# First-layer scores: three half-height products on two 64-row tiles, two query tiles at a time, instead of two full-height products

## The chip, the core and the metric

The kernel runs on one core of a Trainium2 chip. The metric is device time in microseconds (us) of one execution. The engines are named as the profile names them: PE (TensorE matmuls), PEld (TensorE weight loads), DVE (VectorE), ACT (ScalarE), POOL (GpSimd) and SP (SyncE, whose queue issues every DMA here).

## What is computed

Two layers of a decoder trunk on 2048 tokens of width 1024, in float32. Each layer is `x + W_out(mixer(RMSNorm(x)) * silu(gate))`. Layer 0, which the change touches, is stick-breaking attention with 16 heads of width 64; layer 1 is latent attention with 8 heads. The mixer of layer 0, cut to what matters:

```
z = einsum('bthd,bshd->bhts', q, k) * scale          # scores, contracted over d = 64
mask = s_idx < t_idx
log_fail = where(mask, log_sigmoid(-z), 0)
later = cumsum(log_fail, reverse) - log_fail
a = where(mask, exp(log_sigmoid(z) + later), 0)
o = einsum('bhts,bshd->bthd', a, v)
```

## The kernel before

**Exact parts.** The result must be close to float32, and the PE takes each number as a "high" part (the number rounded to the PE's fp32r type) and a "low" part (what is left). A product of two numbers is then built from products of parts. `split` (L432) makes both parts from a bank of PSUM: ACT writes the high part, DVE subtracts it and writes the low part. `HLS` (L374) names the three products that are kept, high*high, high*low and low*high; `unit` (L486) uses them for the projections.

**Stages of layer 0.** `proj0` (L539) computes, for a pair of heads `hp` (8 pairs) and a group `j` of 512 tokens (4 groups), the query, key, value and gate projections with 24 products of 512 columns each. `attn0` (L589) does the attention of one such stage: for each of the two heads it walks the key groups g from j down to 0, and in each the four query tiles `rt` of 128 rows. In the diagonal group (g = j) tile rt needs (rt + 1) * 128 key columns, in the others all 512. There are 64 diagonal and 96 other (head, j, g) blocks, so 640 tiles of scores. For each tile: the score products into a PSUM bank `z` (3 banks), two sigmoids on ACT (L606, L607; the second one overwrites z), a scan along the row on DVE that reads z (L610 or L613), a product on POOL (L615), transposes on the PE into bank `t` (L625), and a split into `at` (L627). After four tiles come the products with the values into bank `av` (L632).

**The scores before.** For a head, `qd` (L552) holds the query's high part in all 128 partitions (64 computed, 64 copied by a DMA, L556) and likewise its low part; `ks` (L558) holds the key's high part in one half of the partitions and its low part in the other half. So one product with a full 128-row contraction gives q_part * k_high + q_part * k_low, and two of them give all four products of parts:

```
z = bank("z")
with sched.group():
    for l in range(2):
        C.mm(z[:, :W], qd[:, h, l, rt * P:(rt + 1) * P], ks[:, h, :W], l == 0, l == 1, W)
```

**Order.** Nothing is written in its final order. The code records instructions, and `Sched.issue` (L185) puts them in an order per engine: it takes, again and again, the instruction that by its own table of durations can start first, among those whose inputs are ready and whose buffers are free. Instructions of one `group` are issued together. `proj0` of the next stage gets priorities that spread it over `attn0` of the current one (L710), so that the PE's queue mixes projection products with attention. The engines then run these orders as they stand, each waiting at the head of its own queue.

**Buffers around it.** The normalised inputs `xn` of a stage (8 slices of 512 KB) come from DRAM through a ring of `XB` = KD + 2 = 10 buffers (L496); in the last projection of a stage the loads for the next one are recorded, two at once and then one after each slice (L573 to L579). During the last attention stage the eight slices of the output weights `wo` are loaded and split (L708), the first 512-token group's `y` is loaded, and the first output tiles are computed between the attention's instructions. Tiles of `x` come in as `xr` (L796). At the layer's other border, eight slices `xk` are loaded for layer 1's input projections; three of them have their own ring `xk0` (L820), five take the place of the output weights.

Of the kernel before, what the change touches and what calls it, by code (L numbers as in the profile page):

```python
# [20 lines left out]
P = 128  # L21
# [10 lines left out]
class Ref:  # L32
    """A view of a buffer that is resolved when its instruction is issued."""

# [28 lines left out]
class Buf:  # L63
    """A tile; with a ring it gets its slot when the first instruction that uses it is issued."""

# [17 lines left out]
class Pool:  # L83
    """A pool that opens over the pools `below`, once the work in the pools `after` has been issued."""

# [30 lines left out]
class Ring:  # L116
    """The slots of a tag, taken in the recorded order; another may go ahead if it leaves `spare` slots free."""

# [9 lines left out]
class Sched:  # L128
    """Puts the recorded instructions in an issue order: each engine takes the first that can run."""

# [11 lines left out]
    def add(self, eng, dur, call, outs, ins):  # L142
        """One instruction; those of a group are issued together."""
        op = self.cur
        if not isinstance(op, Op):
            op = Op()
            op.eng, op.dur, op.calls, op.deps, op.succ, op.bufs = eng, 0.0, [], set(), [], []
            op.idx = op.prio = len(self.ops)
            op.ready = 0.0
            op.lat = self.LAT[eng]  # L150
            self.ops.append(op)
            if self.cur is not None:
                self.cur = op
        op.dur += dur
        op.calls.append(call)
        for refs, write in ((ins, False), (outs, True)):
            for r in refs:
                b = r.buf
                hit = lambda box: all(x0 < y1 and y0 < x1 for (x0, x1), (y0, y1) in zip(box, r.box))  # noqa: E731
                for box, o in b.writes:  # L160
                    if o is not op and hit(box):
                        op.deps.add(o)
                if write:
                    for box, o in b.reads:
                        if o is not op and hit(box):
                            op.deps.add(o)
                if b.ring is not None and b not in op.bufs:
                    op.bufs.append(b)
                    b.left += 1
                    b.ring.pool.left += 1  # L170
                (b.writes if write else b.reads).append((r.box, op))
        return op
# [7 lines left out]
    def spread(self, a, b, lo, hi):  # L180
        """The instructions a..b get priorities that lie evenly between those of lo and hi."""
        for i in range(a, b):
            self.ops[i].prio = lo + (i - a + 0.5) / max(b - a, 1) * (hi - lo)
# [104 lines left out]
class Chip:  # L288
    """The instructions in use, recorded with what they take."""

# [68 lines left out]
    def select(self, x, base, fill):  # L359
        """Keeps x where row + base >= column."""  # L360
        self.s.add("pool", 300.0,
# [16 lines left out]
def trunk(ctx: ExitStack, tc: tile.TileContext, x, w0, wo0, g0, g1, wlat, wgate, gqa, gkva,  # L378
# [33 lines left out]

# [1 line left out]
    ident = const.tile([P, P], F32, "ident")  # L414
    identb = const.tile([P, P], BF16, "identb")
    sched.add("pool", 1000.0, lambda: make_identity(nc, R(ident)), refs(ident), [])
    def causal(dst, base, fill):
        """0 where the column comes before the row (or is at it, base 0), else `fill`."""
        mtmp = pa.tile([P, G], F32, "tmp", 2)[:, 0:P]
# [10 lines left out]

# [1 line left out]
    def split(hi, lo, src, n=G, gain=None):  # L432
# [17 lines left out]
    def norm_scale(pl, xts, jtag, jbufs, mixed=False):  # L450
        """x / rms(x); mixed: with all engines, where nothing else runs."""
        for i in range(4):
# [33 lines left out]
    def unit(acc, w, xk, n=G, after=None):  # L486
        """acc += w^T x over the model width, in three products of exact parts."""
        for k in range(KD):
# [5 lines left out]

# [1 line left out]
    XB = KD + 2  # L496
    ws, kv, xq, cur = {}, {}, {}, {}
# [23 lines left out]
    def load_x(j):  # L521
# [3 lines left out]
        else:  # L525
            xts = [pk.tile([P, D], F32, ("ks", "vv")[i % 2], 5).all() for i in range(4)]
        for i in range(4):
# [11 lines left out]
    def proj0(n):  # L539
# [11 lines left out]
        acc = mul(0)  # L551
        qd = pk.tile([P, 2, 2, G], F32R, "qd", 2)  # L552
        for h in range(2):
            lo_, hi_ = slice(64 * h, 64 * h + 64), slice(64 - 64 * h, 128 - 64 * h)
            split(qd[lo_, h, 0, :], qd[lo_, h, 1, :], acc[lo_, :])
            C.dma(qd[hi_, h].bitcast(F32), qd[lo_, h].bitcast(F32), 256)  # L556
        acc = mul(1)
        ks = pk.tile([P, 2, G], F32R, "ks", 5)  # L558
        for h in range(2):
            lo_, hi_ = slice(64 * h, 64 * h + 64), slice(64 - 64 * h, 128 - 64 * h)  # L560
            split(ks[lo_, h, :], ks[hi_, h, :], acc[lo_, :])
        acc = mul(2)
# [26 lines left out]
    def attn0(hp, j):  # L589
        qd, gt = cur[hp, j]  # L590
        y = pa.tile([P, G], F32, "y")
        for h in range(2):
            av = bank("av")
            prev = {}
            for g in range(j, -1, -1):
                ks, vv = kv[hp, g]
                diag = g == j
                at = pa.tile([P, 2, 4, G], F32R, "at", 2)
                for rt in range(4):
                    W = (rt + 1) * P if diag else G  # L600
                    z = bank("z")
                    with sched.group():
                        for l in range(2):
                            C.mm(z[:, :W], qd[:, h, l, rt * P:(rt + 1) * P], ks[:, h, :W], l == 0, l == 1, W)
                    a = pa.tile([P, G], F32, "a", 5)
# [83 lines left out]
    for n, (hp, j) in enumerate(stages):  # L689
# [11 lines left out]
        else:  # L701
            qy = pk.tile([P, 2, 2, G], F32R, "qd", 2)
            parts = [pk.tile([P, 2, G], F32R, t, 5).all() for t in ("ks", "vv")] + [qy[:, 0], qy[:, 1]]
            for k in range(KD):
                t = parts[k] if k < 4 else pm.tile([P, 2, G], F32R, "y", 4).all()
                C.dma(t.bitcast(F32), y_d[0, :, k], 512)
                yts[0, k] = t
            load_wo(pm, wo0, 0, KD, G // 2, 3)  # L708
            a1 = a0 + int(LAST * (a1 - a0))
# [3 lines left out]

# [1 line left out]
    def out_proj(i, yt, xt, after=None, order=range(KD), dst=None):  # L715
        """x += y wo; with dst the halves of the width go one after the other, each to DRAM as soon as it is there."""
        acc = [bank("pj" if i % 2 == 0 else "z") for _ in range(2)]
# [44 lines left out]
    sk = pb.tile([P, NT, 64], F32, "sk")  # L762

    def prep():
        C.dma(gq_n, gqn, 1)
# [22 lines left out]
    for j in range(NG):  # L788
        done = []
        for i in range(4):  # L790
            t = 4 * j + i
            if t == 1:
                early = [yts[0, k] for k in range(KD)]
                for k in range(4):
                    yts[0, k] = load_y(pl, y_d, 0, k, "y", 4)
            xt = (pl if t else pm).tile([P, D], F32, "xr", 6 if t else 1)  # L796
            C.dma(xt, x[t * P:(t + 1) * P, :], 512)
# [81 lines left out]

# [1 line left out]
    ISQ = 1.0 / math.sqrt(QK1)  # L881
# [34 lines left out]

    def proj1(n):  # the first stages also take the banks that attention leaves free at that time
        h, j = stages[n]
# [142 lines left out]

# [1 line left out]
    pf = sb("pf", "right", (pw1,))  # L1063
# [89 lines left out]
```

## Time and profile before

| | us |
|---|---|
| median of 3 runs | 3069.71 (3065.83 to 3071.62) |
| span of the profiled execution | 3068.7 |
| PE busy in it | 2993.4 |
| PEld busy | 2490.3 |
| DVE busy | 2020.7 |
| ACT busy | 1871.9 |
| POOL busy | 1493.9 |

The median lies 1.0 us above the span of the profiled execution. Layer 0's projections and attention take the first half of the span, to about 1590 us; then come layer 0's output projection, layer 1's input projections (to about 2030 us), layer 1's attention and its output projection. A busy share of the PE tells that matmuls were in flight, not that it ran at its peak; how far apart matmuls of a kind start is read from the timeline.

### The profile page before, as it was taken

Reading aid. Unit: us, or ns where it says so; the run is one execution under the profiler, and the core shown is the slowest. Engines: PE = TensorE matmul, PEld = TensorE weight load, DVE = VectorE, ACT = ScalarE, POOL = GpSimd, SP = SyncE. Lnnn points to the kernel's source line nnn. Section 1 sums busy time; section 2 is a strip of 40 time slices with the busy share of each in tenths; the row PEclk is TensorE's granted clock in tenths of the full one; section 3 lists DMA queues with packets and bytes.
Section 4 is the critical chain, followed back from the end, with each engine's and each line's share of the span. In section 5 each row is a group of like instructions: output and inputs, shape, how many; then the busy total and the mean of one; then the engine's idle time right before and its main releaser. Section 6 shows DMA issues by size and latency. Waiting matters only on the chain.

```text
span 3068.7 us, 48665 instructions
## 1 busy us (share of the span) xinstructions
PE 2993.4 (98%) x15856; PEld 2490.3 (81%) x15856; DVE 2020.7 (66%) x3427; ACT 1871.9 (61%) x4635; POOL 1493.9 (49%) x2931
## 2 busy tenths in 40 slices
PE   8899999999999999999989999989999999999999
PEld 6678888888888888888778888878888888888787
DVE  5777896978869778787863231147777777778511
ACT  5676786867768677786852132257776776777300
POOL 4664664756647565574652120136455455455200
PEclk9899999999999999999999999999999999999999
DMA  6253434344243342433339672142232232223462
GB/s 240 103 172 124 131 104 140 108 138 148 84 147 103 124 152 88 147 121 116 117 121 325 244 276 108 72 157 80 78 95 68 88 103 67 69 80 93 162 216 103
DMA packets 134797, 399.88 MB, mean 130 GB/s; under 512 B 16656, under 2 KB 39696, under 8 KB 131984
## 3 DMA queue, kind: packets, MB, share of 16 engines
q1 hardware_dynamic: 134544, 396.76, 38.4%
q8 instruction: 127, 2.08, 0.3%
q14 instruction: 126, 1.03, 0.1%
HBM read 272.97 MB, written 98.57 MB: 121 GB/s over the span
## 4 chain that ended last, share of the span: by engine, by line
PE 78%; DVE 10%; ACT 5%; issue 3%; POOL 2%; DMA 2%; SPq 0%; DVEq 0%; POOLq 0%; ACTq 0%
PE pj L297 30%; PE z L297 22%; PE av L297 12%; PE t L301 10%; DVE pp L342 3%; PE t L297 3%; PE pj L301 1%; DVE at L319 1%; DVE nm L349 1%; ACT a L312 1%; DVE qs L329 1%; POOL s L329 1%; ACT s L312 1%; DVE y L319 1%; DVE pt L319 1%
## 5 line engine op out<-in xcount | busy, mean ns | idle before, releaser
L297 PE MATMUL pj<-xn,w 128*128 128x512 f32 x3072 | 864.2, 402 | 2.0 <-DVE qd L319 1.9
L319 POOL TENSOR_TENSOR a<-a,pp 128x512 f32<-128x512 f32 (+3 forms) x640 | 612.8, 960 | 475.1 <-DVE pp L342 443.3
L297 PEld LDWEIGHTS pj<-xn,w 128*128 128x128 f32 x3072 | 545.8, 189 | 100.2 <-issue 3.7
L342 DVE TENSOR_TENSOR_SCAN pp<-z,cy,a 128x512 f32<-128x512 f32 x384 | 484.2, 1274 | 43.8 <-ACT z L312 40.8
L312 ACT ACTIVATE at<-t 128x512 fp32r<-128x512 f32 (+3 forms) x640 | 341.0, 535 | 156.9 <-PE t L301 155.0
L319 DVE TENSOR_TENSOR at<-t,at 128x512 fp32r<-128x512 f32 (+3 forms) x640 | 377.7, 599 | 83.6 <-ACT at L312 78.4
L312 ACT ACTIVATE a<-z 128x512 f32<-128x512 f32 (+3 forms) x640 | 335.6, 535 | 117.6 <-PE z L297 101.4
L297 PE MATMUL z<-ks,qd 128*128 128x512 f32 (+3 forms) x1280 | 366.1, 377 | 13.6 <-DVE pp L342 9.5
L297 PE MATMUL av<-at,vv 128*128 128x512 f32 (+3 forms) x1280 | 376.7, 379 | 2.1 <-DVE at L319 2.1
L301 PE MATMUL t<-ident,a 128*128 128x128 f32 x2176 | 344.9, 274 | 8.4 <-POOL a L319 3.6
L301 PEld LDWEIGHTS t<-ident,a 128*128 128x128 f32 x2176 | 272.8, 141 | 82.6 <-POOL a L319 7.2
L312 ACT ACTIVATE z<-z 128x512 f32<-128x512 f32 (+3 forms) x640 | 337.9, 535 | 0.7
L329 POOL TENSOR_SCALAR s<-s,c,ri 128x512 f32<-128x512 f32 (+3 forms) x280 | 200.6, 730 | 164.9 <-DVE ri L353 122.6
L297 PEld LDWEIGHTS z<-ks,qd 128*128 128x128 f32 x1280 | 225.2, 190 | 67.0 <-DVE pp L342 21.5
L297 PE MATMUL av<-pt,vv 128*128 128x512 f32 (+2 forms) x960 | 268.6, 386 | 5.5 <-DVE pt L319 5.3
L312 ACT ACTIVATE s<-z,nm 128x512 f32<-128x512 f32 (+2 forms) x320 | 199.9, 626 | 119.3 <-DVE nm L349 112.5
L297 PE MATMUL z<-knt,qn 128*128 128x512 f32 (+2 forms) x960 | 258.8, 378 | 6.8 <-ACT s L312 6.4
L319 DVE TENSOR_TENSOR pt<-t,pt 128x512 fp32r<-128x512 f32 (+1 forms) x312 | 182.8, 606 | 110.9 <-ACT pt L312 108.4
L297 PEld LDWEIGHTS av<-at,vv 128*128 128x128 f32 x1280 | 223.8, 190 | 38.5 <-DVE at L319 5.5
L342 DVE TENSOR_TENSOR_SCAN pp<-z,later 128x128 f32<-128x128 f32 (+3 forms) x256 | 204.2, 814 | 47.6 <-ACT z L312 30.5
L349 DVE TENSOR_REDUCE nm<-z 128x1 f32<-128x512 f32 (+2 forms) x320 | 190.7, 604 | 38.8 <-PE z L297 37.5
L312 ACT ACTIVATE pt<-t 128x512 fp32r<-128x512 f32 (+1 forms) x312 | 162.0, 533 | 66.4 <-PE t L301 64.6
(234 smaller groups left out, 4940.1 us busy)
## 6 DMA issues: line engine op xcount, KB each, us to landing
xn<-xn_d SPq DMA_DIRECT2D x224, 512.0 KB, 4.8
xn_d<-xn SPq DMA_DIRECT2D x64, 512.0 KB, 3.8
y_d<-yh SPq DMA_DIRECT2D x64, 512.0 KB, 2.6
y<-y_d SPq DMA_DIRECT2D x60, 512.0 KB, 5.0
qd<-qd SPq DMA_DIRECT2D x64, 256.0 KB, 3.0
xk<-xn_d SPq DMA_DIRECT2D x32, 512.0 KB, 6.2
cqt<-c_d SPq DMA_DIRECT2D x16, 1024.0 KB, 5.1
ckv<-c_d SPq DMA_DIRECT2D x32, 512.0 KB, 3.6
```

The lines of the kernel that those rows point to most:

```text
L297: lambda: self.nc.tensor.matmul(R(out), lhsT=R(l), rhs=R(r), start=start, stop=stop),
L301: self.s.add("pe", 109.0, lambda: self.nc.tensor.transpose(R(out), R(src), R(ident)), refs(out), refs(src, ident))
L312: self.nc.scalar.activation(R(out), R(src), func, **kw)
L319: self.s.add(eng, ns, lambda: self.eng[eng].tensor_tensor(out=R(out), in0=R(a), in1=R(b), op=op), refs(out), refs(a, b))
L329: self.s.add(eng, ns, lambda: self.eng[eng].tensor_scalar(out=R(out), in0=R(a), scalar1=R(s1), scalar2=R(s2), op0=op0, op1=op1), refs(out) ...
L342: lambda: self.nc.vector.tensor_tensor_scan(R(out), R(a), R(b), initial=R(init), op0=ALU.mult, op1=op),
L349: lambda: self.nc.vector.tensor_reduce(out=R(out), in_=R(src), axis=AX.X, op=op, **kw),
```

## The change

The scores use two 64-row tiles of the PE's array. `qd` now holds, for even query tiles, both parts of the query in partitions 0 to 63, and for odd query tiles in partitions 64 to 127. `ks` holds both parts of the key in the lower 64 partitions and again in the upper 64; so it is twice as large, and the copying DMA is now that of `ks`. For each pair of query tiles two banks `z` are taken, and six products of 64 rows are issued in one group: for each of the three of `HLS`, one of the lower tile for the even query tile and one of the upper tile for the odd one. The query's parts are split by four instructions of 256 columns per part instead of two of 512. The product low*low is no longer formed.

To make room, the ring of `xn` has 9 buffers instead of 10; the last slice of `wo` is no longer loaded with the others but into two buffers of `xk0`, once the pools of the attention are closed; and the first tile `xr` comes from that later pool too.

```
@@ layer 0 @@
-    XB = KD + 2
+    XB = KD + 1
...
@@ proj0 @@
         acc = mul(0)
-        qd = pk.tile([P, 2, 2, G], F32R, "qd", 2)
+        qd = pk.tile([P, 2, 2, 2, P], F32R, "qd", 2)
+        av_ = acc.all().rearrange("p (a b t) -> p a b t", a=2, b=2)
+        for h in range(2):
+            for b in range(2):
+                r_ = slice(64 * b, 64 * b + 64)
+                split(qd[r_, h, 0], qd[r_, h, 1], av_[64 * h:64 * h + 64, :, b, :], G // 2)
+        acc = mul(1)
+        ks = pk.tile([P, 2, 2, G], F32R, "ks", 5)
         for h in range(2):
             lo_, hi_ = slice(64 * h, 64 * h + 64), slice(64 - 64 * h, 128 - 64 * h)
-            split(qd[lo_, h, 0, :], qd[lo_, h, 1, :], acc[lo_, :])
-            C.dma(qd[hi_, h].bitcast(F32), qd[lo_, h].bitcast(F32), 256)
-        acc = mul(1)
-        ks = pk.tile([P, 2, G], F32R, "ks", 5)
-        for h in range(2):
-            lo_, hi_ = slice(64 * h, 64 * h + 64), slice(64 - 64 * h, 128 - 64 * h)
-            split(ks[lo_, h, :], ks[hi_, h, :], acc[lo_, :])
+            split(ks[lo_, h, 0], ks[lo_, h, 1], acc[lo_, :])
+            C.dma(ks[hi_, h].bitcast(F32), ks[lo_, h].bitcast(F32), 256)
         acc = mul(2)
...
@@ attn0 @@
+                zs = {}
                 for rt in range(4):
                     W = (rt + 1) * P if diag else G
-                    z = bank("z")
-                    with sched.group():
-                        for l in range(2):
-                            C.mm(z[:, :W], qd[:, h, l, rt * P:(rt + 1) * P], ks[:, h, :W], l == 0, l == 1, W)
+                    if rt % 2 == 0:
+                        zs = {r: bank("z") for r in (rt, rt + 1)}
+                        with sched.group():
+                            for n, (lq, lk) in enumerate(HLS):
+                                for r in (rt, rt + 1):
+                                    w = (r + 1) * P if diag else G
+                                    p = slice(64 * (r % 2), 64 * (r % 2) + 64)
+                                    C.mm(zs[r][:, :w], qd[p, h, lq, r // 2, :], ks[p, h, lk, :w], n == 0, n == 2, w / 2)
+                    z = zs[rt]
...
@@ last stage @@
-            load_wo(pm, wo0, 0, KD, G // 2, 3)
+            load_wo(pm, wo0, 0, KD - 1, G // 2, 3)
...
@@ layer 0 out @@
+    wo[KD - 1] = [[], []]
+    for n in range(2):
+        part = pb.tile([P, 2, G], F32R, "xk0", 3)
+        for c in range(0, G, G // 2):
+            raw = pm.tile([P, G // 2], F32, "woraw", 3)
+            C.dma(raw, wo0[:, KD - 1, n * G + c:n * G + c + G // 2], 128)
+            split_sb(part[:, 0, c:c + G // 2], part[:, 1, c:c + G // 2], raw, G // 2, "dve" if c else "pool")
+        for b in range(2):
+            wo[KD - 1][b].append(part[:, b, :])
...
-            xt = (pl if t else pm).tile([P, D], F32, "xr", 6 if t else 1)
+            xt = pl.tile([P, D], F32, "xr", 6)
```

The built program has 16496 matmuls instead of 15856. 1920 of them are 64-row products; they stand in the PE's queue in 320 runs of six, each with full-height matmuls before and behind it.

The PE's queue late in layer 0's attention, in the stage before the last (z: scores, t: transposes, av: products with the values, pj: projections, `ident` the identity of a transpose). Before:

```order
L297 MATMUL pj<-xn,w 128x512 x3
L301 MATMUL t<-ident,a 128x128 x4
L297 MATMUL pj<-xn,w 128x512 x3
L297 MATMUL av<-at,vv 128x512 x2
L301 MATMUL t<-ident,a 128x128 x4
L297 MATMUL av<-at,vv 128x512 x2
L297 MATMUL z<-ks,qd 128x512 x2
L297 MATMUL av<-at,vv 128x512 x2
```

Now:

```order
L301 MATMUL t<-ident,a 128x128 x4
L297 MATMUL z<-ks,qd 128x512 x6
L297 MATMUL pj<-xn,w 128x512 x3
L301 MATMUL t<-ident,a 128x128 x4
L297 MATMUL pj<-xn,w 128x512 x3
L297 MATMUL av<-at,vv 128x512 x2
L297 MATMUL pj<-xn,w 128x512 x3
L297 MATMUL av<-at,vv 128x384 x2
```

Where two products of one query tile stood, six products of two query tiles stand, with as much other work between one such group and the next.

The PE's queue at the end of layer 0's attention, from the last products with the values (`wo`: slices of the output weights; z and pj are here banks of the output projection). Before:

```order
L297 MATMUL z<-wo,y 128x512 x6
L297 MATMUL av<-at,vv 128x512 x2
L297 MATMUL z<-wo,y 128x512 x6
L297 MATMUL pj<-wo,y 128x512 x6
L297 MATMUL z<-wo,y 128x512 x6
L297 MATMUL pj<-wo,y 128x512 x36
```

Now (`xk_19902` and `xk_19911` are the two buffers of the last slice of `wo`):

```order
L297 MATMUL av<-at,vv 128x512 x2
L297 MATMUL z<-wo,y 128x512 x6
L297 MATMUL av<-at,vv 128x512 x2
L297 MATMUL pj<-xk_19902,y 128x512
L297 MATMUL pj<-xk_19911,y 128x512
L297 MATMUL pj<-xk_19902,y 128x512
L297 MATMUL pj<-xk_19911,y 128x512
```

Before, a run of products with slices that are long loaded follows the last `av`; now the first product behind it needs the slice that is loaded last.

SP's queue at the end of layer 0's output projection (`x_d`: finished rows to DRAM; `wgraw`: gate weights of layer 1). Before:

```order
L370 DMA x_d<-xr 128x1024
L370 DMA xk<-xn_d 128x1024 x3
L370 DMA x_d<-xr 128x1024
L370 DMA xk<-xn_d 128x1024 x2
L370 DMA wgraw<-in_wgate_dram 128x512 x4
```

Now:

```order
L370 DMA x_d<-xr 128x1024 x2
L370 DMA xk<-xn_d 128x1024 x3
L370 DMA xk_21212<-xn_d 128x1024
L370 DMA x_d<-xr 128x1024
L370 DMA xk_21226<-xn_d 128x1024
L370 DMA xk<-xn_d 128x1024 x2
L370 DMA wgraw<-in_wgate_dram 128x512 x4
```

The loads of slices 1 and 2 of `xk` (`xk_21212`, `xk_21226`), which were issued long before this place, stand here now among those of slices 3 to 7.

## Rows read from the trace of the kernel before

**Rows 1.** The page's part 1: busy time, share of the span and instructions.

```profile
PE 2993.4 (98%) x15856; PEld 2490.3 (81%) x15856; DVE 2020.7 (66%) x3427; ACT 1871.9 (61%) x4635; POOL 1493.9 (49%) x2931
```

**Rows 2.** Stretches: length, busy PE, PEld, DVE, ACT, POOL, clock, DMA share, GB/s.

```profile
500.00:700.00 200.00, 199.00 (x1062) 165.27 (x1060) 161.77 (x212) 148.17 (x317) 122.97 (x281) 1.00 0.36 116
...
1500.00:1600.00 100.00, 88.84 (x442) 68.94 (x440) 80.71 (x102) 70.76 (x156) 67.72 (x133) 0.98 0.32 106
...
760.10:819.50 59.40, 59.40 (x324) 49.41 (x323) 54.08 (x68) 50.33 (x105) 42.41 (x93) 1.00 0.34 106
819.50:857.80 38.30, 38.30 (x202) 32.09 (x201) 27.41 (x40) 22.80 (x51) 18.17 (x44) 1.00 0.29 95
```

**Rows 3.** Timeline of PE in layer 0's attention: start, length, engine, line, operation.

```profile
705.01 0.62 PE L297 MATMUL z<-ks,qd 128*128 128x512 f32 x2
705.47 0.51 PE L297 MATMUL av<-at,vv 128*128 128x384 f32 x2
705.82 0.86 PE L297 MATMUL pj<-xn,w 128*128 128x512 f32 x3
706.52 0.39 PE L297 MATMUL av<-at,vv 128*128 128x256 f32 x2
706.75 0.63 PE L297 MATMUL z<-ks,qd 128*128 128x512 f32 x2
707.22 0.33 PE L297 MATMUL av<-at,vv 128*128 128x128 f32 x2
707.39 0.90 PE L297 MATMUL pj<-xn,w 128*128 128x512 f32 x3
```

**Rows 4.** Timeline of PE: transposes, and products behind them.

```profile
702.27 0.60 PE L301 MATMUL t<-ident,a 128*128 128x128 f32 x4
702.62 0.95 PE L297 MATMUL pj<-xn,w 128*128 128x512 f32 x3
703.41 0.60 PE L301 MATMUL t<-ident,a 128*128 128x128 f32 x4
...
1630.25 1.04 PE L301 MATMUL t<-ident,xr 128*128 128x128 f32 x8
```

**Rows 5.** Groups by shape: count, busy us, mean ns, idle before them and what ended it.

```profile
L297 PE MATMUL pj<-xn,w 128*128 128x512 f32 x3072 | 864.2, 402 | 2.0 <-DVE qd L319 1.9
...
L297 PE MATMUL z<-ks,qd 128*128 128x512 f32 x896 | 284.1, 410 | 7.6 <-DVE pp L342 5.8 <-ACT wo L312 0.6 <-ACT a L312 0.4
```

**Rows 6.** Timeline of PE in the last attention stage: two scores, the second behind a wait.

```profile
1518.27 0.62 PE L297 MATMUL z<-ks,qd 128*128 128x512 f32 x2
1519.29 0.73 PE L297 MATMUL z<-ks,qd 128*128 128x512 f32 x2 [0.40 <-DVE pp L342]
```

**Rows 7.** Timeline of PE at the end of layer 0's attention.

```profile
1590.93 0.61 PE L297 MATMUL av<-at,vv 128*128 128x512 f32 x2
...
1595.46 2.88 PE L297 MATMUL pj<-wo,y 128*128 128x512 f32 x12
1600.28 6.08 PE L297 MATMUL pj<-wo,y 128*128 128x512 f32 x24 [1.94 <-DMA y<-y_d]
```

**Rows 8.** Groups by shape (end of a stage), and a DMA group: KB, us to landing.

```profile
L319 POOL TENSOR_TENSOR yh<-y,yh 128x512 fp32r<-128x512 f32 x64 | 82.8, 1293 | 137.7 <-ACT yh L312 96.5 <-DVE pp L342 27.1 <-issue 13.0
...
L319 DVE TENSOR_TENSOR y<-av,y 64x512 f32<-64x512 f32 x64 | 43.7, 683 | 83.0 <-ACT y L312 82.6
...
L312 ACT ACTIVATE yh<-y 128x512 fp32r<-128x512 f32 x64 | 40.1, 627 | 14.5 <-DVE y L319 7.4 <-issue 6.7 <-DMA y_d<-yh 0.2
...
L312 ACT ACTIVATE y<-av 64x512 f32<-64x512 f32 x64 | 38.0, 594 | 64.6 <-PE av L297 63.5
...
woraw<-in_wo_dram SPq DMA_DIRECT2D x32, 128.0 KB, 2.1
```

**Rows 9.** Timeline of PE at layer 1's first projection, and that projection's loads.

```profile
1762.38 10.61 PE L297 MATMUL z<-wl,xk 128*128 128x448 f32 x51
...
xk<-xn_d SPq DMA_DIRECT2D x32, 512.0 KB, 6.2
```

More of the change, by code (lines that the diff above doesn't have):

```diff
@@ L525, in load_x @@
         else:
-            xts = [pk.tile([P, D], F32, ("ks", "vv")[i % 2], 5).all() for i in range(4)]
+            xts = [t.all().rearrange("p a b g -> p (a b g)")[:, 0:D] if i % 2 == 0 else t.all()
+                   for i, t in enumerate(pk.tile([P, 2, 2, G] if i % 2 == 0 else [P, D], F32, ("ks", "vv")[i % 2], 5)
+                                         for i in range(4))]
         for i in range(4):
@@ L701, in trunk @@
         else:
-            qy = pk.tile([P, 2, 2, G], F32R, "qd", 2)
-            parts = [pk.tile([P, 2, G], F32R, t, 5).all() for t in ("ks", "vv")] + [qy[:, 0], qy[:, 1]]
+            yk = pk.tile([P, 2, 2, G], F32R, "ks", 5)
+            parts = [yk[:, 0], yk[:, 1], pk.tile([P, 2, G], F32R, "vv", 5).all(), pk.tile([P, 2, G], F32R, "qd", 2).all()]
             for k in range(KD):
```

## The prediction

> **What bounds the kernel now.** I read the busy times first: the PE is busy for 2993.4 of 3068.7 us, the next engine, DVE, for 2020.7 [rows 1]. Then the stretches, since the change touches only layer 0's attention: in 200 us of it the PE is busy for 199.0, DVE for 161.8, ACT for 148.2 [rows 2]. So there a microsecond taken off the PE is a microsecond off the span, as long as DVE does not become the bound. It is near in one kind of stage: the attention of the last 512 tokens (760.1 to 819.5, one of eight alike) has DVE busy for 54.08 of 59.40 us, the stage after it only for 27.41 of 38.30 [rows 2]. Third, the last attention stage and the border behind it, where no projections are left to fill the PE: 88.84 busy of 100 [rows 2]. Busy time overstates a matmul, since they overlap; prices come from start to start in the timeline.
>
> **Prices on the PE.** Two scores of 512 columns take 705.01 to 705.47, so 0.23 us each; two products of 384 columns 0.35 (0.175 each), two of 256 columns 0.23 (0.115 each) [rows 3]. For 128 columns I take 0.11: eight transposes last 1.04 and four 0.60, so four more cost 0.44 [rows 4]. As 128 and 256 columns cost nearly the same, something that does not depend on the columns sets a floor there; each product brings a load of 128 weight columns, and I read 0.11 as its price.
>
> **1. The scores themselves: -38.4 us.** An off-diagonal block has four tiles of two products of 512 columns, 8 x 0.23 = 1.84. After the change it has two groups of six. If the lower and the upper tile run side by side, a group takes three products' time, 3 x 0.23 = 0.69; its six weight loads, if they come one after the other, take 6 x 0.11 = 0.66, just hidden. Two groups are 1.38, so 0.46 saved, in 96 blocks 44.2 us. A diagonal block now takes 2 x (0.11 + 0.115 + 0.175 + 0.23) = 1.26. After: the group of 128 and 256 columns is bound by its loads, 0.66, the group of 384 and 512 columns by its longer product, 0.69, so 1.35: 0.09 lost in 64 blocks, 5.8 us. The sum is -38.4. No row shows two tiles of the array at work, so both ends stay: if the loads run side by side too, the first diagonal group takes 3 x 0.115 = 0.345 and the sum is 20 us better (-58); if nothing runs side by side it is the second rival below. I take the middle since the floor of 0.11 is in the rows.
>
> **2. Going from full height to half height and back: 0, up to 173 us.** The 320 groups of six stand alone between full-height work, so there are 640 such changes. The nearest thing in the trace is the change between transposes and products: four transposes and three products behind them take 702.27 to 703.41, 1.14, and by the prices 0.44 + 0.69 = 1.13 [rows 4]. It costs nothing, so I take 0. It is not the same thing, since both use all 128 rows. From above: if the PE had to empty before each change, a product would start at the end of the one before rather than 0.23 after its start. A pair of 512 columns lasts 0.62, so a single one 0.39: 0.16 lost; and a pair that starts behind a wait lasts 0.73 instead of 0.62 [rows 6], 0.11 more. Together 0.27 a change, 173 us. Below zero it can't go: a change removes no work. The break-even of the whole sum is 18.4 / 640 = 0.029 us a change.
>
> **3. What DVE takes back: +10 us (0 to 21).** Of the 38.4, a stage of the last 512 tokens has 6 off-diagonal and 2 diagonal blocks: 6 x 0.46 - 2 x 0.09 = 2.6 us, eight stages 21 us. There the PE's need falls to 56.8 while DVE has 54.1 of work, and a little more now: the query's parts are made by twice as many instructions of half the width, at most another 2 x 0.68 us on DVE and 2 x 0.59 on ACT a stage, by the row of the same 64x512 shape [rows 8]. DVE would have to be busy for about 96% of the stage. Also, a group needs two of the three banks z free at once, where one was enough; waits of scores for DVE's scan cost the PE 5.8 us now [rows 5]. I take half of the 21 as lost. In the other stages DVE's slack (10 of 38 us [rows 2]) covers the added splits.
>
> **4. The end of layer 0: +5 us (0 to 9).** After the last product with the values (starts at 1590.93) the PE has work until it waits 1.94 us for the reloaded y, to 1600.28 [rows 7]. Now the next products need the last slice of wo, which is split once the attention's pools close: behind y's way through ACT (0.59), DVE (0.68, twice), ACT (0.63) and POOL (1.29) [rows 8], 3.9 us. The fourth part of the slice is loaded only then, behind three other issues; with a landing of 2.1 [rows 8] and its split I come to some 8.7 us of waiting. Then come 12 products on that slice and 12 that stood before 1600.28, 5.5 us: 14.2 instead of 8.9. The products that were moved ahead go into a stretch where the PE waits anyway (11 of 100 us [rows 2]).
>
> **5. The start of layer 1's projections: +4 us (0 to 6).** 51 products (10.6 us) on the first three slices xk cover the load of the others [rows 9]. Now two of these three slots hold wo until its last use, so slices 1 and 2 are loaded with the rest. Their landing takes 6.2 us [rows 9]; the PE has about 2 us of products on slice 0 in the meantime.
>
> **6. One buffer less for xn: +1 us (0 to 20).** The loads for the next stage start one slice later, at least 0.69 us of products. The projections have waited 2.0 us in all, for DVE and for no load [rows 5]; lost leads of 0.7 in all of 28 stages would be 20 us. The copying DMA moves from the query to the key: as many, as large, and with the value and gate projections (48 x 0.23 = 11 us) to cover it.
>
> **Sum.** -38.4 + 0 + 10 + 5 + 4 + 1 = -18.4: the profiled execution goes from 3068.7 to 3050.3, and with the 1.0 us by which the median lies above it to **3051 us** (0.6% faster).
>
> **Rivals.**
>
> *The PE empties at each change of height* (slower). For it: nothing in the trace has half-height work, so nothing shows that the next product may follow at the usual 0.23. Against it: transposes and products follow each other free [rows 4]. It decides from 0.029 us a change. With the refill alone (0.11 [rows 6]) it costs 70 us; PE and not DVE is then the bound in every stage, so term 3 falls away: 3069.7 - 38.4 + 70 + 10 = 3112. With the full 0.27 it is 3215. I take 3112 as its time, 3076 to 3215 as its bounds.
> By the Trainium skill, "TensorEngine Tiling (Array Packing)", section Key Properties, changing the tiling mode drains the TensorE, while changing from tile to tile within a mode does not. It names no price; no run so far shows it, and by it the sum would be this rival's.
>
> *The two tiles don't run side by side* (the change doesn't do what it says). Then a group of six takes six times: off-diagonal 12 x 0.23 = 2.76 instead of 1.84, diagonal 3 x (0.11 + 0.115 + 0.175 + 0.23) = 1.89 instead of 1.26: 88 + 40 us more, with terms 4 to 6 about 3208. The rows neither speak for it nor against it: all products there use the whole height.
>
> *DVE and the borders eat the gain.* Term 3 in full (21), waits for pairs of banks twice what they are (+8), the borders at 9: -38.4 + 38 = 0, about 3070.
>
> **How the numbers follow.** The forecast's own case gets 0.44; its range is 3032 (a part of the loads side by side, nothing lost to DVE) to 3063. The emptying PE gets 0.36, since half-height work is a larger step than a transpose, and most of its prices lie above break-even. Tiles one after the other: 0.07. An eaten gain: 0.13. About 0.2% (6 us) is what a measurement of this kernel can tell from no change. Faster by more than that, below 3063.6, is the first case, 0.44; within it is the last, 0.13; slower the two others, 0.43. For 8 in 10 the range must reach far into the emptying PE, to 0.185 us a change (118 us): 3069.7 - 38.4 + 118 + 10 = 3160. Above it lie the tiles one after the other and the dearest changes, below 3032 a few per cent.
>
> **What would show it.** In the timeline after, a row of six scores of 512 columns and the row behind it start 0.69 us apart (forecast), about 1.4 (no side by side), and 0.8 to 1.2, with as much lost at the row behind, if changes cost. Term 3: in a stage of the last 512 tokens PE waits for DVE's scan, and DVE is busy for over 95%. Terms 4 and 5: waits of some 9 us before the first product on the last slice of wo, and of some 4 before the second slice of layer 1's first projection. The prediction is wrong first of all if the change of height has a price, as everything else is small beside 640 times it.

## The result, and the profile after

The changed kernel takes **3175.12 us** (median of 3 runs, 3171.3 to 3176.93) against 3069.71: a ratio of 1.0339, with a 95% interval of 1.0325 to 1.0354. It is 105 us slower. The forecast was 3051, and the range ended at 3160: the prediction was wrong in its direction, and the time lies above its range.

The first parts of the page after (busy us, share of the span, instructions) and the scores' widest form (busy us, mean ns of one, idle time before them and what ended it), to be held against [rows 1, 5]:

```profile
span 3175.2 us, 49694 instructions
PE 3073.8 (97%) x16496; PEld 2427.0 (76%) x16496; DVE 2030.9 (64%) x3491; ACT 1881.9 (59%) x4699; POOL 1499.5 (47%) x2931
...
L297 PE MATMUL z<-ks,qd 64*128 64x512 f32 x1344 | 259.4, 433 | 6.3 <-DVE pp L342 6.1
```

DVE, ACT and POOL have about the busy time that they had. The PE is busy for 80 us more, and the span is 106 longer: most of the time went into the PE itself. The group row of the scores hardly tells where: a half-height product of 512 columns lasts 433 ns on the mean, a full one lasted 410 [rows 5]. What a matmul costs is read from start to start. The timeline of the PE after, in layer 0's attention (start, length, engine, line, operation):

```profile
704.98 0.62 PE L297 MATMUL z<-ks,qd 64*128 64x128 f32 x6
705.53 0.65 PE L301 MATMUL t<-ident,a 128*128 128x128 f32 x4
...
713.43 3.73 PE L297 MATMUL pj<-xn,w 128*128 128x512 f32 x15
717.09 0.97 PE L297 MATMUL z<-ks,qd 64*128 64x512 f32 x6
717.99 0.96 PE L297 MATMUL pj<-xn,w 128*128 128x512 f32 x3
718.79 0.49 PE L301 MATMUL t<-ident,a 128*128 128x128 f32 x3
```

The six scores from 717.09 take 0.90 to the next start, not the 0.69 of the forecast. The three products behind them take 0.80 (717.99 to 718.79), where three in full-height surroundings take 0.70 [rows 3]. The fifteen ahead take 3.66 where 15 x 0.23 is 3.45; they stand between two groups, so both ends of a group show in them. From the starts of all 114 groups of six 512-column scores with such products on both sides, I took the medians: the first score starts 0.326 after the product ahead of it, its partner on the other tile 0.004 later, the second pair 0.338 after the first, the third 0.231 after the second. The first full-height product starts 0.32 after the third pair, and the one behind it 0.337 later. A step without a change is 0.231. So four steps are each about a tenth of a microsecond too long: into the change and behind it, on either side of the group. Together that is **0.40 us a group, or 0.20 a change**, and for 320 groups 128 us. The groups of 128 and 256 columns, and of 384 and 512, come to the same 0.40: the price doesn't depend on the width inside.

The weight loads (PEld) show what these steps are made of. Here are the loads at the same two changes (in brackets PEld's idle time before them, for which the profile shows no wait), and below them those of a group of three full-height scores in the first experiment, whose products start at 702.83:

```profile
717.09 0.53 PEld L297 LDWEIGHTS z<-ks,qd 64*128 64x128 f32 x6 [0.35 <-issue]
717.99 0.53 PEld L297 LDWEIGHTS pj<-xn,w 128*128 128x128 f32 x3 [0.37 <-issue]
...
702.61 0.65 PEld L612 LDWEIGHTS z<-ks,qd 128*128 128x128 f32 x3
```

Where the height stays, the load for a product starts 0.003 after the product ahead of it and 0.23 before its own (medians of full-height products of 512 columns): it is hidden. At each of the 640 changes, in either direction, it starts at most 0.003 before its own product; behind a full-height product of 512 columns that is 0.32 after it started. The load behind it starts 0.11 later, and the second product is late by as much. So of the 0.20 a change about half is the time until a load may start, and half the load itself, which nothing hides.

The waits of the PE after (what waited for what; us in all, times, longest):

```profile
PE t L301 <- POOL a L319: 16.1, 18, 3.5
PE pj L297 <- ACT xk L312: 10.6, 2, 7.2
...
PE pj L297 <- DVE qd L319: 8.7, 10, 2.2
PE z L297 <- DVE pp L342: 6.6, 17, 1.2
PE z L297 <- DMA xk<-xn_d: 6.1, 3, 5.0
```

The scores' own wait for DVE's scan did not grow (6.6; before, the whole was 10.2, in a row below). Two waits at the borders are new in size: 10.6 us for the last slice of `wo` (in a buffer named `xk` now) where 1.94 had been waited for `y` [rows 7], and 6.1 for slices of layer 1's `xk`, where 0.5 had been waited. The timeline there shows what stands behind them:

```profile
1676.16 0.61 PE L297 MATMUL av<-at,vv 128*128 128x512 f32 x2
1680.18 0.69 PE L297 MATMUL pj<-xk,y 128*128 128x512 f32 x1 [3.41 <-ACT xk L312]
1688.03 2.50 PE L297 MATMUL pj<-xk,y 128*128 128x512 f32 x5 [7.15 <-ACT xk L312]
1690.33 2.76 PE L297 MATMUL z<-xk,y 128*128 128x512 f32 x6
...
1866.17 4.82 PE L297 MATMUL z<-wl,xk 128*128 128x448 f32 x12 [5.03 <-DMA xk<-xn_d]
```

And the same places as stretches (length; busy PE, PEld, DVE, ACT, POOL; granted clock; DMA share; GB/s):

```profile
1688.00:1692.00 4.00, 3.97 (x9) 3.14 (x10) 1.71 (x3) 0.54 (x1) 0.00 (x0) 0.50 1.02 414
1696.00:1700.00 4.00, 4.00 (x19) 3.30 (x18) 0.16 (x1) 0.00 (x0) 2.17 (x3) 1.00 0.88 281
1866.00:1871.00 5.00, 4.83 (x14) 4.23 (x15) 0.00 (x0) 0.00 (x0) 1.12 (x1) 0.50 1.02 410
```

After each long wait the granted clock stands at 0.50, the 1.2 GHz level, and the products come half as often: twelve of 448 columns take 4.62 (1866.17 to 1870.79), where 51 took 10.61 in [rows 9], 0.21 each and 2.5 for twelve.

### The profile page after: what moved, and what is told of

It is laid out like the page before. It is cut to its first block, busy times and chain, and to the rows that moved or that the text cites. A ratio compares the mean times of both kernels' runs of the same rounds, so it can differ in the third digit from the quotient of the medians.

```text
span 3175.2 us, 49694 instructions
## 1 busy us (share of the span) xinstructions
PE 3073.8 (97%) x16496; PEld 2427.0 (76%) x16496; DVE 2030.9 (64%) x3491; ACT 1881.9 (59%) x4699; POOL 1499.5 (47%) x2931
## 4 chain that ended last, share of the span: by engine, by line
PE 82%; DVE 7%; ACT 4%; issue 3%; POOL 2%; DMA 2%; SPq 0%; POOLq 0%; DVEq 0%; ACTq 0%
PE pj L297 33%; PE z L297 22%; PE av L297 12%; PE t L301 10%; PE t L297 3%; PE pj L301 1%; DVE pp L342 1%; DVE nm L349 1%; ACT s L312 1%; POOL s L329 1%; DVE at L319 1%; DVE pt L319 1%; DVE qs L329 1%; DVE qd L319 1%; POOL a L319 1%
## 5 line engine op out<-in xcount | busy, mean ns | idle before, releaser
L297 PEld LDWEIGHTS pj<-xn,w 128*128 128x128 f32 x3072 | 537.2, 189 | 143.9 <-issue 49.5
L312 ACT ACTIVATE a<-z 128x512 f32<-128x512 f32 (+3 forms) x640 | 315.9, 532 | 197.0 <-PE z L297 183.1
L297 PE MATMUL av<-at,vv 128*128 128x512 f32 (+3 forms) x1280 | 387.7, 390 | 1.1 <-ACT at L312 0.5
L312 ACT ACTIVATE z<-z 128x512 f32<-128x512 f32 (+3 forms) x640 | 329.4, 533 | 0.4
L297 PE MATMUL z<-ks,qd 64*128 64x512 f32 (+3 forms) x1920 | 302.0, 401 | 7.3 <-DVE pp L342 6.6
L297 PEld LDWEIGHTS z<-ks,qd 64*128 64x128 f32 x1920 | 161.3, 187 | 119.3 <-issue 74.0
```

What stands on the lines that cost most here:

```text
L297: lambda: self.nc.tensor.matmul(R(out), lhsT=R(l), rhs=R(r), start=start, stop=stop),
L312: self.nc.scalar.activation(R(out), R(src), func, **kw)
```

## The experiments

Theory A is that the change of height has a price of its own, some 0.20 us, whatever the group does. Theory B is that the two tiles disturb each other, or that the extra waits come from the engines around the PE. The rest concerns the smaller terms. Code is shortened; `...` marks what is left out. Each kernel is the changed one unless it says "before".

### Three full-height products in place of the six

```
-    for r in (rt, rt + 1):
...
-        C.mm(zs[r][:, :w], qd[p, h, lq, r // 2, :], ks[p, h, lk, :w], n == 0, n == 2, w / 2)
...
+    matmul(zs[rt + (n > 0)][:, :w], qd[:, h, lq, rt // 2, :], ks[:, h, lk, :w])   # 128 rows
```

> The changed kernel with three full-height products for each pair of query tiles in place of six half-height ones: no change of height is left, everything else (order of all engines, buffers, DMAs) is that of the changed kernel. The scores are then not those of the reference (a product over 128 rows sums two query tiles), so it only tells time. Theory A (each change between full and half height costs the PE about 0.20 us, 640 of them): 3175 less 320 x 0.40 = 3047, up to 3062 if DVE takes some back; a group of three of 512 columns and the next row start 0.69 to 0.72 us apart. Theory B (the loss sits in the order, the banks taken in pairs and the room made): above 3120, with more waits of the PE than in the changed kernel.

Measured: **3071.83 us** (3069.28 to 3074.57), ratio to before 1.0007 (0.9998 to 1.0016). The 320 groups, their banks, the splits and the borders are all there; only the height of the products, and with it their number, is another, and 103 us are gone. (The number is not what costs: in a group of six the third pair starts 0.231 after the second, the pace of single full-height products.) The timeline of this kernel's PE:

```profile
702.83 0.85 PE L612 MATMUL z<-ks,qd 128*128 128x512 f32 x3
703.52 0.62 PE L297 MATMUL av<-at,vv 128*128 128x512 f32 x2
703.99 0.85 PE L297 MATMUL pj<-xn,w 128*128 128x512 f32 x3
704.67 0.51 PE L297 MATMUL av<-at,vv 128*128 128x384 f32 x2
```

The three scores take the 0.69 of the forecast, and the products behind them keep their pace (0.47 for two, 0.68 for three). That is theory A. It missed in two respects: the time is above the 3047 to 3062 that I had expected, and the difference to the changed kernel is 103, not 129. At least half of the missing 26 us went into waits for the engines behind the scores:

```profile
PE t L301 <- POOL a L319: 22.1, 21, 3.8
PE pj L297 <- DVE qd L319: 13.4, 16, 2.2
PE pj L297 <- ACT xk L312: 10.2, 2, 6.8
PE z L612 <- DVE pp L342: 10.1, 22, 1.4
```

The first, second and fourth rows sum to 45.6 here and to 31.4 in the changed kernel, 14 us: a PE that is done sooner waits longer for POOL, for the query's split and for the scan. So with changes of height at no price at all, this kernel would still have been as slow as before.

### More changes in the same groups

A small full-height product of zeros in bf16, 64 columns wide, behind the first two of the six; and as its control the same product behind the first of the three above.

```
     C.mm(zs[r][:, :w], qd[p, h, lq, r // 2, :], ks[p, h, lk, :w], n == 0, n == 2, w / 2)
+    if n == 0:
+        matmul(zs[rt][:, 0:64], later[:, 0:P], identb[:, 0:64])        # 128 rows, zeros
```

> The changed kernel with one small full-height product (64 columns, zero weights, added to the first bank) behind the first two of each six half-height products: the changes of height are doubled to 1280, the scores stay the same. Theory A: 320 x 0.40 = 129 us more for the changes and 20 to 35 for the product itself (as in the control): 3320 to 3345; the difference to the control is 258. Theory B: about 3195 to 3210, the product's own time alone; the difference to the control is that of the changed kernel to the run with three full-height products.

> The run with three full-height products, with the same small full-height zero product behind the first of each three: what that product costs where it changes no height. As in that run the scores are not those of the reference. Both theories: 20 to 35 us above the run with three full-height products (0.06 to 0.11 us each); by A that is 3067 to 3097.

Measured: **3284.63** (3280.87 to 3285.61) and **3093.61** (3090.85 to 3097.55). The control came as expected, 22 us above the kernel without the small product. The other is 109.5 above the changed kernel, short of the 145 and more of theory A and far above the 35 at most of theory B. Net of the small product, 640 more changes cost 191 - 103 = 88 us, 0.14 each and not 0.20. The timeline of the kernel with the product in the middle, and below it a group of the control:

```profile
706.37 0.49 PE L297 MATMUL z<-ks,qd 64*128 64x512 f32 x2
706.80 0.20 PE L617 MATMUL z<-identb,later 128*128 128x64 bf16 x1
706.93 0.73 PE L297 MATMUL z<-ks,qd 64*128 64x512 f32 x4
707.59 0.96 PE L297 MATMUL pj<-xn,w 128*128 128x512 f32 x3
...
709.60 0.40 PE L612 MATMUL z<-ks,qd 128*128 128x512 f32 x1
...
710.42 0.63 PE L297 MATMUL av<-at,vv 128*128 128x512 f32 x2
```

From 706.37 to 707.59 there are 1.22, 0.32 more than the 0.90 above; the small product takes 0.13 of that in the control (709.60 to 710.42, 0.82 instead of 0.69). The next half-height product starts only 0.13 after the small one. Either a short product leaves less to lose, or a second change close behind the first is cheaper. Two more kernels told these apart: the same edit with a product of the scores' type, as wide as those of the even tile.

```
+    if n == 0:
+        matmul(zs[rt][:, :v], qd[:, h, 0, rt // 2, :], ks[:, h, 0, :v])        # 128 rows
```

> The changed kernel with one more full-height product in each of the 320 groups, behind its first two half-height ones, of the even query tile's width (512 columns in 192 groups, 128 or 384 in the rest); it adds q_high times k_high of both tiles to the scores, so the scores are other numbers. It makes 640 more changes of height; the product itself takes 0.23 of 512 columns, some 62 us in all (192 x 0.23 + 64 x 0.11 + 64 x 0.175). Theory A (a change costs 0.20 whenever full products stand on one side of it; the cheaper second round trip of the run with a 64-column product came from that product being short): a group of 512 columns takes 1.09 + 0.23 + 0.40 = 1.72, the time is 3175 + 62 + 128 less up to 20 that the engines behind the scores give back: 3345 to 3365. Theory B (a second round trip close behind the first costs only half, whatever stands between): 1.52 to 1.55, and 3295 to 3315.

> The run with three full-height products for each pair of query tiles, and the same additional product: four full-height products in a group, no change of height; the scores are sums over two query tiles. Both theories: a group of 512 columns takes 0.92 instead of 0.69; 62 us more work on the PE than with three products, of which up to 26 go into waits for DVE and POOL that it had: 3108 to 3134. The difference to the kernel with the changes in the middle is 103 + 128 = 231 by theory A, 103 + 65 to 88 by theory B.

Measured: **3354.04** (3351.42 to 3362.53) and **3111.32** (3107.52 to 3114.91), both inside theory A's intervals; the difference is 243, so 640 more changes cost 243 - 103 = 140 us, 0.22 each. The timeline of the kernel with the wide product in the middle:

```profile
707.36 0.49 PE L297 MATMUL z<-ks,qd 64*128 64x512 f32 x2
707.78 0.50 PE L617 MATMUL z<-ks,qd 128*128 128x512 f32 x1
708.22 0.73 PE L297 MATMUL z<-ks,qd 64*128 64x512 f32 x4
708.88 0.96 PE L297 MATMUL pj<-xn,w 128*128 128x512 f32 x3
709.68 0.60 PE L301 MATMUL t<-ident,a 128*128 128x128 f32 x4
```

The group takes 1.52 to the next product's start (707.36 to 708.88), and the three behind it 0.80 again. Of the 0.62 above the changed kernel's 0.90, 0.23 are the product and 0.39 the two changes. The price is 0.20 a change with products of full length on both sides, also four times within 2 us. So it is not nearness that made the changes around the small product cheaper; whether its length or its type did, these runs do not tell apart.

### The other order within a group

Three products of the lower tile, then three of the upper.

```
-    for n, (lq, lk) in enumerate(HLS):
-        for r in (rt, rt + 1):
+    for r in (rt, rt + 1):
+        for n, (lq, lk) in enumerate(HLS):
```

> The changed kernel with the six products in another order: the three of the lower tile first, then the three of the upper tile; as many changes of height. If the tiles take their products strictly in the queue's order, only the third and the fourth run side by side: a group of 512 columns gets 2 x 0.23 = 0.46 us longer, in all some 120 us more (3285 to 3305). If the queue could run ahead of a busy tile, 3175 as before this edit.

Measured: **3173.53** (3170.94 to 3174.9), the time of the changed kernel. Of the two outcomes that I had named this is the second: the tiles don't work strictly in the queue's order. A diagonal group shows it: its lower tile has 384 columns, its upper tile 512, and in the queue the three of 384 stand first. The groups of PE instructions that start in 712.0 to 712.2 of this kernel (busy, mean ns, idle before):

```profile
L297 PE MATMUL z<-ks,qd 64*128 64x512 f32 x1 | 0.5, 497 | 0.0
L297 PE MATMUL z<-ks,qd 64*128 64x384 f32 x1 | 0.4, 442 | 0.0
```

The first of the upper tile has started beside the first of the lower one, ahead of two that stand before it in the queue. So the six run as three pairs in either order, and the time behind the change is not an effect of the order in the queue.

### The room alone

The kernel before with the smaller ring of `xn`, the late last slice of `wo` and the late `xr`, its scores untouched.

```
-    XB = KD + 2
+    XB = KD + 1
...
-            load_wo(pm, wo0, 0, KD, G // 2, 3)
+            load_wo(pm, wo0, 0, KD - 1, G // 2, 3)
```

> The kernel before with only the room made: 9 buffers of xn, the last slice of the output weights loaded late, all xr tiles from the later pool; scores as before. Theory A with the border waits of the changed kernel's trace (10.6 us in place of 1.9 at the end of layer 0, 6.1 in place of 0.5 at layer 1's first projection, and a lower clock behind each): 3088 to 3094. The forecast's terms for this were 10 us: 3080. Theory B: above 3110.

Measured: **3088.12** (3084.84 to 3090.23), ratio 1.0058 (1.0042 to 1.0075): **19.6 us** for what the forecast had priced at 10 in its terms 4, 5 and 6. The waits of its PE, and the stretch around the first:

```profile
PE pj L297 <- ACT xk L312: 10.2, 2, 6.8
...
PE z L297 <- DMA xk<-xn_d: 5.5, 3, 4.7
```

```profile
1580.00:1610.00 30.00, 19.77 (x72) 15.39 (x71) 7.42 (x12) 4.30 (x9) 5.43 (x8) 0.77 0.55 204
```

The waits are 10.2 and 5.5, near the 8.7 and 4 of the forecast. What it left out is the clock behind them. The granted clock is 0.77 on the mean of these 30 us: it stands at 0.50, the 1.2 GHz level, for 13.7 of them (1592.0 to 1605.7), in which the PE waits for 6.8 and works for 6.8, and again for 6.8 (1776.3 to 1783.2), in which it works for 5.7. At half the pace the working time lost some 3.4 and 2.8 us. With the 8.3 and 5.0 by which the two waits outlast those of before (1.94 and 0.5), that is about the whole 19.6. The layer up to its last projection is as long as before within 2 us, so the smaller ring costs next to nothing.

### Pairs of query tiles, at full height

The kernel before, with the four products of two query tiles in one group, and nothing else.

```
-    z = bank("z")
-    with sched.group():
-        for l in range(2):
-            C.mm(z[:, :W], qd[:, h, l, rt * P:(rt + 1) * P], ks[:, h, :W], l == 0, l == 1, W)
+    if rt % 2 == 0:
+        zs = {r: bank("z") for r in (rt, rt + 1)}
+        with sched.group():
+            for r in (rt, rt + 1):
+                for l in range(2):
+                    C.mm(zs[r][:, :w], qd[:, h, l, r * P:(r + 1) * P], ks[:, h, :w], l == 0, l == 1, w)
```

> The kernel before with the scores of two query tiles issued as one group (four full-height products, two banks taken at once): the coupling of banks alone, without half height and without the room made. Theory A: within 6 us of before (3064 to 3076). Theory B: 15 us or more above before, with more waits of the PE for DVE's scan and for POOL.

Measured: **3100.0** (3097.05 to 3103.08), ratio 1.0096 (1.0081 to 1.0111). The pairs alone cost **30 us**, where theory A had at most 6: on this point theory B's forecast, 15 or more, came true. The PE does the same products, and waits more:

```profile
PE t L301 <- POOL a L319: 12.1, 17, 2.4
...
PE z L297 <- DVE pp L342: 9.1, 16, 3.0
...
PE pj L297 <- DMA y<-y_d: 7.4, 1, 7.4
...
PE av L297 <- DVE at L319: 4.1, 11, 0.6
```

In the kernel before, the first two of these rows read:

```profile
PE z L297 <- DVE pp L342: 10.2, 20, 1.4
...
PE t L301 <- POOL a L319: 3.6, 3, 2.4
```

The wait for the scan (`pp`) is not among what grew. The transposes wait for POOL's product, the products with the values for their split, and at the end of the layer the PE waits 5.5 us longer for `y` (7.4 instead of 1.94 [rows 7]). Two tiles that start together reach each engine behind the scores together, and the third bank can't take a group alone; that this is the mechanism is argued from the rows and was not tested. Some ten of the 30 us have no row that I could name.

### Half the changes

With four banks for z and one for the projections, and the output projection on z's banks alone: groups of six (the control) and groups of twelve, all four query tiles at once.

```
-        bufs, spare = {"z": (3, None), "t": (2, 1), "av": (1, None), "pj": (2, 1)}[tag]
+        bufs, spare = {"z": (4, None), "t": (2, 1), "av": (1, None), "pj": (1, None)}[tag]
...
-                    if rt % 2 == 0:
-                        zs = {r: bank("z") for r in (rt, rt + 1)}
+                    if rt == 0:
+                        zs = {r: bank("z") for r in range(4)}
...
-        acc = [bank("pj" if i % 2 == 0 else "z") for _ in range(2)]
+        acc = [bank("z") for _ in range(2)]
```

> The changed kernel with four banks for scores and one for projections (and the output projection on score banks only): a control for the next run. Both theories: the groups of six and their 640 changes stay; 3165 to 3200, depending on what the single projection bank costs.

> As the control with four score banks, but twelve half-height products for all four query tiles of a block in one group: 160 groups and 320 changes instead of 640. Theory A: 160 x 0.40 = 64 us less than the control (55 to 70, if the coarser groups make no new waits). Theory B: the same as the control or slower, since four banks are now taken at once.

Measured: **3399.5** (ratio 1.1073, 1.1057 to 1.109) and **3426.41** (1.1159, 1.1141 to 1.1178). The control was expected at 3165 to 3200. These banks cost it some 225 us: 53.0 us of waits for the query's split alone, where there were 8.7. In that surrounding twelve at once are 27 us slower than six, not 64 faster. On the PE the saving is there. The timeline of the kernel with twelve:

```profile
746.82 0.60 PE L301 MATMUL t<-ident,a 128*128 128x128 f32 x4
747.35 1.66 PE L297 MATMUL z<-ks,qd 64*128 64x512 f32 x12
748.93 0.65 PE L301 MATMUL t<-ident,a 128*128 128x128 f32 x4
```

The twelve take 1.58 to the next start, two groups of six 0.90 each. But the transposes wait 44.7 us for POOL's product in this kernel and 9.4 in its control (second row):

```profile
PE t L301 <- POOL a L319: 44.7, 50, 2.4
...
PE t L301 <- POOL a L319: 9.4, 9, 2.4
```

So whether fewer changes would pay with enough banks can't be read from these two times; what four tiles at once cost behind the PE is more than what two changes give back. No version that I ran beats the kernel before.

## Why the prediction was wrong

**Term 2, the change of height: this is the step that failed.** I took 0, from transposes and products that follow each other free, and held 0.27 for the upper end. The runs show 0.20 in the timeline and 103 us net for the whole kernel (against three full-height products), of 128 on the PE. The break-even of 0.029 was right by the forecast's own terms, and so was the sentence that this term outweighs the others. What went wrong was the choice between the two ends: the row that I took as nearest has the same height on both sides of the change, and I had said so. A change for which no row exists should not have been given the price of one in which the height stays. The bound from above did better: its 0.11 for the refill is what the step behind a change loses (0.11, the weight load), and its 0.16 for the emptying stands against 0.10 on the step into it.

**The rival "the PE empties"** is what happened, by its price and by the weight loads that start late; that the array is empty at that moment no row shows. I had chosen its lower price, the refill alone (0.11, 3112); the measured price gives 3069.7 - 38.4 + 128 + 10 = 3169 by its own sum. Its range of prices held 0.20, but the range on record was cut at 0.185. The Trainium skill, "TensorEngine Tiling (Array Packing)", section Key Properties, says that a change of the tiling mode drains the TensorE; the trace agrees in so far as each change costs 0.20 us.

**Term 1, the scores.** The mechanism was right: the tiles start 0.004 apart and three half-height pairs take the time of three products. The size was off to the good side. The weight loads of the two tiles also run side by side (they start 0.003 apart): in the group of 128 and 256 columns the third pair starts 0.12 after the second, so without its changes the group takes 0.36, not 0.66. That is near the term's other end, -58 instead of -38.4; by the starts in the traces, 192 x (0.92 - 0.69) + 64 x (0.83 - 0.69) + 64 x (0.41 - 0.36) = 56. The 0.41 is below the forecast's own price of 0.45, since 0.11 for a product of 128 columns was too high: already [rows 3] has two of them in 0.17 (707.22 to 707.39). The second rival, tiles one after the other, is excluded by the same rows.

**Term 3, what DVE takes back (10, at most 21).** Too small. The kernel with three full-height products gains 56 us on the scores and loses 20 at the borders, yet it stands 2 us above before; so about 38 went elsewhere, into waits as far as the rows show. If the pairs cost here what they cost alone, 30 of them are theirs. I had looked for them at DVE's scan and in the stages of the last 512 tokens; they came mostly at POOL's product and at the query's split. DVE, which should have been busy for over 95% of such a stage, is busy for 46.6 of 54.8 us in the changed kernel and for 45.9 of 50.5 in the one with three full-height products (793.2 to 848.0 and 749.4 to 799.9, the stretches of the projections that stood at 760.1 to 819.5). In the changed kernel less is lost in this way: of the 105 us, 128 are changes, -56 the scores, 20 the room, which leaves 13. Its PE is later, so the others are ready sooner; that last part is argued.

**Terms 4, 5 and 6 (5, 4 and 1).** 19.6 together. The waits were near their forecast; the lower clock behind them, some 6 us, was left out. Term 5 also misread its row: with three banks z and three products a slice, the first three slices have at most 27 of its 51 products. Term 6 is next to nothing, as said.

**The rival "DVE and the borders eat the gain"** (about 3070) is what the chip gives when the changes are taken out: 3071.83. The forecast's own case, 3051, would not have come about even with changes at no price.

## What to carry to other kernels

Work that uses the array in another tiling should stand in long runs: on the PE a run must gain more than the 0.40 us that going there and back costs, and six products of 512 columns gained 0.23. That longer runs pay in the whole kernel is not shown: the one try, twelve at once, lost more behind the PE. Ask for an operation that no row shows what differs from the nearest row, and if just the disputed property differs, take a price between the bounds rather than the row's. And a group that takes two buffers at once can have a price at the engines behind it, even if it does the same work: 30 us here.

## What was not expected of the hardware

A change between 128-row and 64-row products costs 0.20 us, the same for 128 and for 512 columns inside the group, and some 0.14 where a 64-column product in bf16 stands between. At all 640 changes the weight load started with its product, where it otherwise starts 0.23 ahead. Products of the two row tiles run side by side in whichever order they stand in the queue (3173.5 and 3175.1 us), and so do their weight loads: pairs of 128 and 256 columns come about 0.12 apart. Behind waits of 6.8 and 4.7 us the PE worked for about 6 us more at the 1.2 GHz level, at half its pace, so each cost some 3 us beyond its own length.
